# A two-layer decoder step on one core: the masked softmax copy negated and scaled, the attention blocks in another order, 32-row and 32-column tiles widened to 128, the last sums of squares collected in PSUM

## The chip, the cores and the metric

The kernel runs on one NeuronCore of a Trainium2 chip. Five engines work side by side, each on its own queue: TensorE (PE in the profile; its weight loads are PEld), VectorE (DVE), ScalarE (ACT), GpSimd (POOL) and SyncE (SP), which issues nearly all DMAs. The metric is the device time of one execution in microseconds (us), the median of repeated executions.

## The reference

One step of a small hybrid decoder, D = 1024, for 512 prompt tokens and 8 sequences of 8 sample tokens. What matters, cut:

```
x = x + g1 * (recurrent_block(modulate(rms_norm(x))))        # layer 0
x = x + g2 * swiglu(modulate(rms_norm(x)))
k, v = rope/split(modulate(rms_norm(x)) @ w_kv)               # shared keys and values
q = rope(modulate(rms_norm(x)) @ w_q)                         # layer 1, 16 heads of 64, 4 kv heads
s = where(mask, (q . k) / 8, -1e30)                           # window of 128
m = max(max(s), sink);  e = exp(s - m)
p = e / (sum(e) + exp(sink - m));  o = p @ v
x = x + g1 * (o @ w_o)
x = x + g2 * swiglu(modulate(rms_norm(x)))
y = rms_norm(x)                                               # and the state and k/v windows
```

rms_norm divides by sqrt(mean(x^2) + 1e-6) over the 1024 channels of a token and multiplies by a gain.

## The kernel before, in words

Channels lie on the 128 partitions, tokens on the columns. The tokens are cut into two halves A (h = 0) and B (h = 1) of HC = 288 columns each: 256 prompt tokens and 32 sample tokens (4 sequences of 8). x[h] holds 8 chunks of 128 channels. Every large product splits its operands into a rounded high part and a rest and does three passes of 128x128 weights against 288 columns (product, line 982; the products of the second feed-forward have an own form, lines 1293 and 1351). Those products are most of the program.

The order of all instructions is made when the kernel is built: each call on T, V, S, G or Q (TensorE, VectorE, ScalarE, GpSimd, SyncE) only records an operation with its reads and writes; schedule (line 213) then places the operations one by one, by a table of estimated costs, the place in the record (its priority, which early(n) moves forward by n), and free buffers, at most 24 candidates deep on an engine. All instructions therefore carry line 447, and the groups are told apart by the names of their tiles: mm and ada are PSUM tiles, wh weights, h the normalised input, sl, ta, tb, td working tiles, acc the running sum of squares, tst and stat small statistics.

The places that the change touches:

- stats and spread (lines 793 and 802), run for both halves ahead of the first feed-forward, of the k/v projection and of the second feed-forward; spread also runs twice at the very start. stats sums acc over the channels with three small products against a column of ones (tokens 0 to 127, 128 to 255, and the 32 sample tokens, the last as a 128x32 tile), two VectorE instructions scale them into tst. spread raises them to the power -1/2 on GpSimd and brings them from partitions to columns with three transposes; the third works on a tile of 32 rows.
- The attention stage. Its order is the string ATT (line 53): q0A is the query projection of chunk 0 (two heads) for half A, a0A the attention of that chunk (attn_chunk, line 1566), s0A a block of sample attention (attn_sample, line 1646), fA the end of half A's attention (attn_fin, line 1745, with k_out, line 1726, which writes out new keys), o0A the output projection. A chunk does its scores, the softmax, and leaves transposes and the product with V to a second part that runs one block later. Per chunk VectorE copies four score tiles out of PSUM while it adds the mask, and takes each row's maximum (tensor_tensor_reduce); for each of two column blocks two small instructions make the negated maximum and the sink's exponent (lines 1592 to 1594); then ScalarE's Exp.
- sink_setup (line 1443) prepares the sinks; evac_v (line 1488) transposes the new values, the sample part from a 128x32 tile to partitions 0 to 31.
- The end: final_chunk (line 1787) transposes each finished chunk of x (two 128x128 tiles, one 128x32) and multiplies by the final gain; final_norm (line 1801) squares the last chunk, adds its column sums to those of acc in three PSUM tiles, and then for each of three token tiles scales, raises to -1/2, multiplies the two halves of the row on VectorE and ScalarE, and issues one DMA for each half. square (line 782) adds a chunk's squares to acc on VectorE.
- residual (line 1008) adds a product to x; out (line 1351) runs the last projection of a feed-forward.

Of the kernel before, what the change touches and what calls it, by code (L numbers as in the profile page):

```python
# [52 lines left out]
ATT = ("q0A a0A q1A q2A q0B a1A q1B a0B a2A q3A q2B a1B a3A q3B q4A q4B a2B q5A a4A a3B q6A a5A q5B a4B "  # L53
       "q7A a6A q6B a5B s0A s1A a7A s2A s3A q7B s0B a6B fA a7B o0A s1B s2B o1A s3B o2A fB")
# [419 lines left out]
def trunk_kernel(ctx, tc, a):  # L474
# [17 lines left out]
    def aux():  # L492
        return ps()
# [308 lines left out]
    def spread(h, r0=0):  # L802
# [205 lines left out]
    def residual(h, o, c, g, last):  # L1008
# [6 lines left out]
        if last and (g != L1 + G2 or c < KC - 1):  # L1015
            square(h, c)
# [160 lines left out]
    def ffn(l, g, after):  # L1177
# [173 lines left out]
        def out(k, m, h):  # L1351
# [6 lines left out]
            residual(h, o, m, g, last)  # L1358
# [84 lines left out]
    def sink_setup():  # L1443
        raw, sinks, nsink, sinkS = snk[:, 0:16], snk[:, 16:32], snk[:, 32:48], snk[:, 48:51]
        A["sinks"], A["nsink"], A["sinkS"] = sinks, nsink, sinkS
# [6 lines left out]
        for g in range(2):  # L1452
            V.tensor_copy(sinks.rearrange("p (g l j) -> p g l j", g=2, l=4)[:, g], sv[:, g])
            V.tensor_scalar(nsink.rearrange("p (g l j) -> p g l j", g=2, l=4)[:, g], sv[:, g], -1.0, None, ALU.mult)
        V.tensor_scalar(sinkS[:, 1:2], sinkS[:, 0:1], 8.0, None, ALU.mult)
        V.tensor_scalar(sinkS[:, 2:3], sinkS[:, 0:1], -1.0, None, ALU.mult)
# [31 lines left out]
    def evac_v(gp):  # L1488
        def f(h, o):
# [6 lines left out]
            T.transpose(t[0:32, 2 * P : 3 * P], u.f[:, HP:HC], ident[:])  # L1496
# [7 lines left out]
            V.tensor_copy(vs[h][0:32, gs], t[0:32, 2 * P : 3 * P])  # L1504
            for b in range(4):
                Q.dma_start(
                    a["sample_v"][4 * h + b, P - NT : P].rearrange("t g d -> t (g d)")[:, gs],
                    vs[h][b * NT : (b + 1) * NT, gs],
# [57 lines left out]
    def attn_chunk(c):  # L1566
# [3 lines left out]
        def run(h):  # L1570
# [10 lines left out]
            mx, nm, den, rd = [st[:, 4 * i : 4 * i + 4] for i in range(4)]  # L1581
            e = [(ta(), tb()) for _ in range(2)]
            masks, sinks, nsink = A["masks"], A["sinks"], A["nsink"]
            for b, W in enumerate(wide):
                i = slice(2 * b, 2 * b + 2)
# [416 lines left out]
```

## Time and profile before

| what | value |
|---|---|
| median of 3 runs | 1262.38 us (1261.91 to 1264.16) |
| the profiled execution's own time | 1263.01 us |
| its span, first to last instruction | 1261.2 us |
| TensorE busy | 1237.8 us, 98% of the span |
| VectorE, ScalarE, GpSimd busy | 920.3, 663.1, 252.7 us |
| mean granted TensorE clock | 0.995 |
| chain that ended last | TensorE 86%, VectorE 6%, ScalarE 4%, DMA 2% |

A matmul's end is modelled, and a matmul is in flight while its successors run, so the busy time of TensorE hides small losses; the distance from one start to the next tells what a matmul really holds. The idle time of an engine off the chain costs nothing.

### The profile page before, as it was taken

To read this page: it belongs to the slowest core of one execution; us is meant where nothing else is said; L and a number is where in the kernel's file an instruction comes from. 1 tells how busy PE (TensorE), PEld (TensorE's weight loads), DVE (VectorE), ACT (ScalarE), POOL (GpSimd) and SP (SyncE) were. 2 spreads that over 40 slices of the span, in tenths; PEclk is the share of its full clock that TensorE was granted. 3 is DMA by queue.
4 is the path that set the end of the run, shared out by engine and by line. 5 is a ranking of instruction groups with operands and counts; after the bars stand their busy time and mean duration, and the time that the engine had idled before them with its cause. 6 is when DMAs were issued, how large, how long until landed. Compare 5 with 4: busy or idle time off the path is not lost.

```text
span 1261.2 us, 25276 instructions
## 1 busy us (share of the span) xinstructions
PE 1237.8 (98%) x9532; PEld 1166.9 (93%) x9532; DVE 920.3 (73%) x2283; ACT 663.1 (53%) x1498; POOL 252.7 (20%) x542
## 2 busy tenths in 40 slices
PE   7999999999999999999999999999999999999997
PEld 5798999899899899989998997999999999999997
DVE  6998784795577468656778887558957865875776
ACT  4788973764255335514567678538523542552442
POOL 3456351101100010011024335100011011001011
PEclk8999999999999999999999999999999999999999
DMA  9955554535456655464513220332342232332322
GB/s 306 318 179 188 188 177 151 170 86 171 140 152 191 185 167 184 156 194 137 167 33 75 68 60 27 111 97 97 85 133 68 84 110 76 90 100 80 100 69 76
DMA packets 219755, 165.38 MB, mean 131 GB/s; under 512 B 23629, under 2 KB 204841, under 8 KB 219602
## 3 DMA queue, kind: packets, MB, share of 16 engines
q1 hardware_dynamic: 219186, 163.45, 43.0%
q8 instruction: 75, 1.23, 0.4%
q0 software_dynamic: 448, 0.32, 0.1%
q14 instruction: 46, 0.38, 0.1%
HBM read 160.85 MB, written 4.87 MB: 131 GB/s over the span
## 4 chain that ended last, share of the span: by engine, by line
PE 86%; DVE 6%; ACT 4%; DMA 2%; POOL 1%; issue 1%; SPq 0%; ACTq 0%; DVEq 0%
PE mm L447 82%; PE ada L447 4%; DVE wh L447 1%; DVE ta L447 1%; ACT tb L447 1%; DVE sl L447 1%; ACT ta L447 1%; DVE tb L447 1%; ACT h L447 1%; DMA raw<-in_rnn_w_in_dram 1%; ACT wh L447 1%; POOL h L447 1%; DMA reg<-in_ada_w_dram 1%; ACT sl L447 1%; DMA reg<-in_x_prompt_dram 1%
## 5 line engine op out<-in xcount | busy, mean ns | idle before, releaser
L447 PE MATMUL mm<-h,wh 128*128 128x288 f32 x4128 | 596.2, 298 | 3.8 <-ACT h L447 1.8
L447 PEld LDWEIGHTS mm<-h,wh 128*128 128x128 f32 x4128 | 560.5, 188 | 23.2 <-issue 11.3
L447 PE MATMUL mm<-sl,wh 128*128 128x288 f32 x3218 | 460.6, 296 | 0.4 <-ACT sl L447 0.3
L447 ACT CAST wh<-raw 128x512 fp32r<-128x512 f32 (+2 forms) x380 | 269.1, 721 | 345.7 <-PE mm L447 208.9
L447 PEld LDWEIGHTS mm<-sl,wh 128*128 128x128 f32 x3218 | 436.6, 188 | 9.0 <-issue 5.9
L447 DVE TENSOR_TENSOR wh<-raw,wh 128x512 fp32r<-128x512 f32 (+2 forms) x380 | 310.2, 828 | 59.3 <-ACT wh L447 57.0
L447 DVE SCALAR_TENSOR_TENSOR x<-mm,mods,x 128x256 f32<-128x256 f32 x160 | 77.0, 482 | 136.1 <-PE mm L447 136.0
L447 POOL TENSOR_TENSOR td<-td,td 128x288 f32<-128x288 f32 x38 | 35.5, 934 | 475.8 <-ACT td L447 467.7
L447 POOL TENSOR_TENSOR x<-x,ta 128x32 f32<-128x32 f32 x152 | 55.3, 364 | 331.1 <-DVE ta L447 325.9
L447 PE MATMUL mm<-tb,wh 128*128 128x288 f32 (+1 forms) x488 | 88.5, 296 | 0.4 <-ACT td L447 0.4
L447 PEld LDWEIGHTS mm<-tb,wh 128*128 128x128 f32 x488 | 72.4, 188 | 1.9 <-DVE sl L447 0.8
L447 ACT COPY td<-mm 128x288 f32<-128x288 f32 (+2 forms) x140 | 49.0, 364 | 37.7 <-DVE mm L447 18.0
L447 DVE TENSOR_TENSOR raw<-raw,raw 128x512 f32<-128x512 f32 x76 | 61.4, 808 | 0.9
L447 PE MATMUL mm<-ta,wh 128*128 128x288 f32 (+1 forms) x254 | 56.1, 298 | 0.0
L447 ACT ACTIVATE ta<-x 128x288 f32<-128x288 f32 x56 | 24.8, 444 | 55.6 <-POOL x L447 52.4
L447 DVE TENSOR_TENSOR raw<-raw 128x512 f32<-128x512 f32 x76 | 52.2, 688 | 1.1
L447 DVE TENSOR_TENSOR td<-mm,td 128x288 f32<-128x288 f32 x76 | 34.5, 454 | 23.4 <-PE mm L447 23.3
L447 PE MATMUL ada<-reg,cz 128*32 128x512 f32 (+1 forms) x448 | 49.5, 553 | 0.0
L447 PEld LDWEIGHTS mm<-ta,wh 128*128 128x128 f32 x254 | 41.7, 188 | 1.8 <-ACT wh L447 0.8
L447 ACT ACTIVATE ta<-ta,stat 128x128 f32<-128x128 f32 (+2 forms) x72 | 32.3, 471 | 18.5 <-DVE stat L447 17.7
L447 DVE TENSOR_TENSOR acc<-acc,ta 128x288 f32<-128x288 f32 x54 | 25.1, 464 | 12.4 <-ACT ta L447 12.4
L447 ACT CAST sl<-ta 128x288 fp32r<-128x288 f32 x54 | 23.0, 431 | 18.5 <-DVE ta L447 18.5
(202 smaller groups left out, 1197.9 us busy)
## 6 DMA issues: line engine op xcount, KB each, us to landing
raw<-in_ffn_w_in_dram SPq DMA_DIRECT2D x88, 512.0 KB
reg<-in_ada_w_dram SPq DMA_DIRECT2D x80, 512.0 KB
raw<-in_ffn_w_out_dram SPq DMA_DIRECT2D x48, 384.0 KB
raw<-in_rnn_w_in_dram SPq DMA_DIRECT2D x16, 512.0 KB
reg<-in_kv_ada_w_dram SPq DMA_DIRECT2D x16, 512.0 KB
wh<-in_ada_w_dram SPq DMA_DIRECT2D x24, 256.0 KB
raw<-in_rnn_w_out_dram SPq DMA_DIRECT2D x8, 512.0 KB
raw<-in_ffn_w_out_dram SPq DMA_DIRECT2D x8, 512.0 KB
```

The costliest lines, as they stand in the source:

```text
L447: self.rec.add(eng, lambda: getattr(obj, name)(*map(real, args), **{k: real(v) for k, v in kw.items()}), cost, outs, ins, func, lat, port, ...
```

## The change

Five things, in one diff:

1. In the softmax the masked copy multiplies by -1/8 and takes the minimum, starting from the negated sink (a value per partition, read through a pointer). It so leaves -m itself; the two small VectorE instructions of each column block go, one subtraction for the whole chunk comes, and Exp gets scale -1. In the sample blocks one small instruction goes.
2. The string ATT has another order.
3. Tiles of 32 rows or 32 columns become 128 wide: the third sum in stats, the third transpose in spread, the sample part of the transposes in evac_v, attn_sample and final_chunk. The sample tokens then come out on partitions 96 to 127 (TAIL) instead of 0 to 31, and what reads them follows. stats has one VectorE instruction instead of two.
4. k_out transposes the new keys of both halves and all heads at once (one transpose and one copy instead of four of each).
5. At the end the squares of chunk 6 are no longer added to acc; acc, they and the squares of chunk 7 are summed by nine small products into one PSUM tile. One VectorE instruction scales it, two GpSimd instructions raise it, and each token tile leaves by one DMA instead of two. The last residual and this block move forward by 60 places in the record.

The core of the diff:

```diff
-ATT = ("q0A a0A q1A q2A q0B a1A q1B a0B a2A q3A q2B a1B a3A q3B q4A q4B a2B q5A a4A a3B q6A a5A q5B a4B "
-       "q7A a6A q6B a5B s0A s1A a7A s2A s3A q7B s0B a6B fA a7B o0A s1B s2B o1A s3B o2A fB")
+ATT = ("q0A q1A a0A a1A q2A q0B q1B q2B a0B q3A a2A q4A a3A a1B q3B a2B q5A a4A q4B a3B q6A a5A q5B a4B "
+       "q7A a6A s0A q6B a7A s1A s2A s3A a5B q7B s0B a6B fA o0A s1B a7B s2B s3B o1A o2A fB")
...
-    TOK = [slice(0, P), slice(P, 2 * P), slice(2 * P, HC)]
+    late_square = [None, None]
+
+    TOK, TAIL = [slice(0, P), slice(P, 2 * P), slice(HC - P, HC)], slice(P - 32, P)
...
-            T.matmul(pt[0 : ts.stop - ts.start, t : t + 1], acc[h][:, ts], ones, start=True, stop=True)
-        V.tensor_scalar(st[:, 0:2], pt[:, 0:2], 1.0 / D, EPS, ALU.mult, ALU.add)
-        V.tensor_scalar(st[0:32, 2:3], pt[0:32, 2:3], 1.0 / D, EPS, ALU.mult, ALU.add)
+            T.matmul(pt[:, t : t + 1], acc[h][:, ts], ones, start=True, stop=True)
+        V.tensor_scalar(st, pt[:, 0:3], 1.0 / D, EPS, ALU.mult, ALU.add)
         spread(h)
...
-        for t, ts in enumerate(TOK):
-            r = slice(r0, r0 + 32) if t == 2 else ALL
-            T.transpose(o[:, ts], rs[r, t : t + 1].to_broadcast([r.stop - r.start, P]), ident[r, r])
+        for t, n0 in ((2, HP - r0), (0, 0), (1, P)):
+            T.transpose(o[:, n0 : n0 + P], rs[:, t : t + 1].to_broadcast([P, P]), ident[:])
...
-        if last and (g != L1 + G2 or c < KC - 1):
+        if last and g == L1 + G2 and c == KC - 2:
+            late_square[h] = s = ta()
+            S.activation(s.f[:, 0:HC], x[h][:, c, :], AF.Square)
+        elif last and (g != L1 + G2 or c < KC - 1):
             square(h, c)
...
-            residual(h, o, m, g, last)
+            with early(60 if last and l == 1 and m == KC - 1 else 0):
+                residual(h, o, m, g, last)
...
             for b, W in enumerate(wide):
-                i = slice(2 * b, 2 * b + 2)
                 for j in range(2):
-                    y = e[b][j].f
-                    V.tensor_tensor_reduce(out=y[:, 0:W], in0=sc[j][:, 256 * b : 256 * b + W], in1=masks[:, 256 - W : 256], op0=ALU.add, op1=ALU.max,
-                                           scale=1.0, scalar=-1e30, accum_out=mx[:, 2 * b + j : 2 * b + j + 1])
-                V.scalar_tensor_tensor(nm[:, i], mx[:, i], -0.125, nsink[:, 2 * c : 2 * c + 2], ALU.mult, ALU.min)
-                V.tensor_tensor(mx[:, i], nm[:, i], sinks[:, 2 * c : 2 * c + 2], ALU.add)
+                    k, y = 2 * b + j, e[b][j].f
+                    V.tensor_tensor_reduce(out=y[:, 0:W], in0=sc[j][:, 256 * b : 256 * b + W], in1=masks[:, 256 - W : 256], op0=ALU.add, op1=ALU.min,
+                                           scale=-0.125, scalar=nsink[:, 2 * c + j : 2 * c + j + 1], accum_out=nm[:, k : k + 1])
                 for j in range(2):
-                    y = e[b][j].f[:, 0:W]
-                    S.activation(y, y, AF.Exp, bias=nm[:, 2 * b + j : 2 * b + j + 1], scale=0.125, accum_out=den[:, 2 * b + j : 2 * b + j + 1])
-
-            S.activation(mx, mx, AF.Exp)
-            V.tensor_tensor(den, den, mx, ALU.add)
+                    k, y = 2 * b + j, e[b][j].f[:, 0:W]
+                    S.activation(y, y, AF.Exp, bias=nm[:, k : k + 1], scale=-1.0, accum_out=den[:, k : k + 1])
+            nk2 = nsink[:, 2 * c : 2 * c + 2].unsqueeze(1).to_broadcast([P, 2, 2])
+            V.tensor_tensor(sk.rearrange("p (b j) -> p b j", b=2), nm.rearrange("p (b j) -> p b j", b=2), nk2, ALU.subtract)
+            S.activation(sk, sk, AF.Exp)
+            V.tensor_tensor(den, den, sk, ALU.add)
...
-                T.transpose(t[0:32, P : 2 * P], e.f[:, P:W], ident[:])
+                T.transpose(t[:, P : 2 * P], e.f[:, W - P : W], ident[:])
...
-                V.tensor_copy(pn[:, :, bl, :], t[0:32, P : 2 * P].rearrange("p (g n) -> p g n", g=2))
+                V.tensor_copy(pn[:, :, bl, :], t[TAIL, P : 2 * P].rearrange("p (g n) -> p g n", g=2))
...
     def k_out(h):
+        if h == 0:
+            t = aux()
+            T.transpose(t[:, 0:P], A["nk"].rearrange("p g h n -> p (g h n)"), ident[:])
+            nkT.append(sl())
+            S.copy(nkT[0].f[:, 0:P], t[:, 0:P])
         for gp in range(2):
-            t = aux()
-            T.transpose(t[0:32, 0:P], A["nk"][:, gp, h, :], ident[:])
-            ko_ = sl()
-            ko = ko_.f[0:32, 0:128]
-            S.copy(ko, t[0:32, 0:P])
...
-        T.transpose(t[0:32, 2 * P : 3 * P], x[h][:, c, HP:HC], ident[:])
+        T.transpose(t[:, 2 * P : 3 * P], x[h][:, c, TOK[2]], ident[:])
...
+        for i, r in enumerate((ALL, ALL, TAIL)):
+            V.tensor_tensor(yt[h][i][r, cs], t[r, i * P : (i + 1) * P], gfin[r, cs], ALU.mult)
...
+        with early(60):
+            w = ta()
+            S.activation(w.f[:, 0:HC], x[h][:, KC - 1, :], AF.Square)
+            pt = aux()
+            st, rs = tst[h][:, 0:3], tst[h][:, 3:6]
+            sums = (acc[h], late_square[h].f, w.f)
+            for i, y in enumerate(sums):
+                for t, ts in enumerate(TOK):
+                    T.matmul(pt[:, t : t + 1], y[:, ts], ones, start=i + t == 0, stop=i == 2, skip_group_check=True)
+            late_square[h].done()
+            w.done()
+            V.tensor_scalar(st, pt[:, 0:3], 1.0 / D, EPS, ALU.mult, ALU.add)
+            G.tensor_tensor(rs[:, 0:1], st[:, 0:1], mhalf[:, 0:1], ALU.pow)
+            G.tensor_tensor(rs[:, 1:3], st[:, 1:3], mhalf[:, 1:3], ALU.pow)
         for t in range(3):
...
+            y = yt[h][t][r, :]
+            if t < 2:
+                Q.dma_start(a["y_prompt"][0, h * HP + t * P : h * HP + (t + 1) * P, :], y)
+            else:
+                Q.dma_start(a["y_sample"][4 * h : 4 * h + 4].rearrange("b t d -> (b t) d"), y)
```

## Rows read from the trace of the kernel before

**Rows 1.** Stretches: length, busy us (count) of PE, PEld, DVE, ACT, POOL; clock, DMA, GB/s.

```profile
692.00:770.00 78.00, 76.13 (x666) 68.41 (x666) 65.67 (x279) 57.39 (x190) 32.86 (x73) 1.00 0.22 55
770.00:812.00 42.00, 40.76 (x339) 34.37 (x340) 28.95 (x129) 28.63 (x107) 14.77 (x40) 1.00 0.30 85
812.00:1250.00 438.00, 437.58 (x3298) 435.76 (x3297) 315.06 (x674) 197.56 (x412) 46.70 (x92) 1.00 0.30 90
1250.00:1261.20 11.20, 3.72 (x27) 2.85 (x26) 4.89 (x21) 2.83 (x5) 1.91 (x4) 0.78 0.30 105
```

**Rows 2.** TensorE in order of time (start, length, idle), around one stats and spread.

```profile
843.57 0.69 PE L447 MATMUL mm<-small,acc 128*128 128x1 f32 x6
844.19 1.60 PE L447 MATMUL mm<-h,wh 128*128 128x288 f32 x10
845.63 0.55 PE L447 MATMUL mm<-ident,tst 128*128 128x128 f32 x3
846.11 2.12 PE L447 MATMUL mm<-h,wh 128*128 128x288 f32 x14
```

**Rows 3.** TensorE in order of time, last projection with final_chunk's transposes.

```profile
1246.12 0.38 PE L447 MATMUL mm<-ident,x 128*128 128x128 f32 x2
1246.26 0.77 PE L447 MATMUL mm<-sl,wh 128*128 128x288 f32 x4
1246.87 0.27 PE L447 MATMUL mm<-ident,x 128*32 128x128 f32 x1
1246.90 1.96 PE L447 MATMUL mm<-sl,wh 128*128 128x288 f32 x13
```

**Rows 4.** VectorE in order of time, inside one chunk's softmax.

```profile
723.21 0.16 DVE L447 SCALAR_TENSOR_TENSOR stat<-stat,snk 128x2 f32<-128x2 f32 x1
723.28 0.42 DVE L447 CUSTOM_DVE_ANT_0 tb<-mm,reg 128x256 f32<-128x256 f32 x1
```

**Rows 5.** VectorE groups by shape, 690 to 830: busy us, mean ns, idle before, releasers.

```profile
L447 DVE SCALAR_TENSOR_TENSOR x<-mm,mods,x 128x256 f32<-128x256 f32 x9 | 4.3, 483 | 7.9 <-PE mm L447 7.9
L447 DVE TENSOR_TENSOR h<-ada,h 128x256 fp32r<-128x256 f32 x4 | 1.7, 420 | 0.7 <-ACT h L447 0.6
```

**Rows 6.** Waits of TensorE, 640 to 812: total us, times, longest.

```profile
PE mm L447 <- DVE td L447: 0.5, 2, 0.3
PE mm L447 <- ACT td L447: 0.4, 2, 0.2
```

**Rows 7.** All engines in order of time, the last ten microseconds.

```profile
1251.60 0.18 DVE L447 TENSOR_TENSOR ta<-mm,mods 128x32 f32<-128x32 f32 x1
1251.70 0.28 DVE L447 TENSOR_TENSOR h<-mm,h 128x128 f32<-128x128 f32 x1
...
1252.66 0.17 DVE L447 TENSOR_TENSOR x<-x,ta 128x32 f32<-128x32 f32 x1
1252.92 0.44 ACT L447 ACTIVATE ta<-x 128x288 f32<-128x288 f32 x1 [1.19 <-DVE x L447]
...
1253.42 0.76 PE L447 MATMUL mm<-small,ta 128*128 128x1 f32 x6
1253.48 0.67 DVE L447 TENSOR_TENSOR h<-mm,h 128x128 f32<-128x128 f32 x3 [0.65 <-PE mm L447]
1254.08 0.28 DVE L447 TENSOR_SCALAR tst<-mm 128x1 f32<-128x1 f32 x3
1254.29 1.66 POOL L447 TENSOR_TENSOR tst<-tst,small 128x1 f32<-128x1 f32 x3 [3.03 <-DVE tst L447]
...
1254.88 1.95 ACT L447 ACTIVATE h<-h,tst 128x512 f32<-128x512 f32 x3 [1.51 <-POOL tst L447]
1255.39 1.82 SPq L447 DMA_DIRECT2D out_y_prompt_dram<-h  x4
1257.30 1.16 SPq L447 DMA_DIRECT2D out_y_sample_dram<-h  x2
```

**Rows 8.** GB/s that all DMAs moved, 1255.0 to 1261.2, 40 equal slices of 0.155 us.

```profile
GB/s 0 0 0 0 0 0 0 13 330 383 383 410 331 357 423 396 383 357 383 383 410 384 383 344 396 304 278 251 251 80 0 0 0 0 0 0 0 0 0 0
```

More of the change, by code (lines that the diff above doesn't have):

```diff
@@ L1495, in f @@
                 T.transpose(t[:, b * P : (b + 1) * P], u.f[:, b * P : (b + 1) * P], ident[:])
-            T.transpose(t[0:32, 2 * P : 3 * P], u.f[:, HP:HC], ident[:])
+            T.transpose(t[:, 2 * P : 3 * P], u.f[:, TOK[2]], ident[:])
             u.done()
@@ L1670, in run @@
             st = new_stat()
-            mx, nm, den, rd = st[:, 0:1], st[:, 1:2], st[:, 2:3], st[:, 3:4]
+            nm, den, rd = st[:, 0:1], st[:, 1:2], st[:, 2:3]
             e = ta()
-            V.tensor_tensor_reduce(out=e.f[:, 0:W], in0=o[:, 0:W], in1=masks[:, 256 + W * bl : 256 + W * (bl + 1)], op0=ALU.add, op1=ALU.max,
-                                   scale=1.0, scalar=-1e30, accum_out=mx)
             G.tensor_copy(e.f[:, W : W + 1], sinkS[:, 1:2])
-            V.scalar_tensor_tensor(nm, mx, -0.125, sinkS[:, 2:3], ALU.mult, ALU.min)
-            S.activation(e.f[:, 0 : W + 1], e.f[:, 0 : W + 1], AF.Exp, bias=nm, scale=0.125, accum_out=den)
+            V.tensor_tensor_reduce(out=e.f[:, 0:W], in0=o[:, 0:W], in1=masks[:, 256 + W * bl : 256 + W * (bl + 1)], op0=ALU.add, op1=ALU.min,
+                                   scale=-0.125, scalar=sinkS[:, 1:2], accum_out=nm)
+            S.activation(e.f[:, 0 : W + 1], e.f[:, 0 : W + 1], AF.Exp, bias=nm, scale=-1.0, accum_out=den)
             V.reciprocal(rd, den)
@@ L1697, in second @@
                 for gp in range(2):
-                    T.matmul(av[:, 256 * gp : 256 * gp + 256], vs[h][0:32, gp * P : (gp + 1) * P], pn[:, gp].rearrange("p b n -> p (b n)"), start=False, stop=True, skip_group_check=True)
+                    T.matmul(av[:, 256 * gp : 256 * gp + 256], vs[h][TAIL, gp * P : (gp + 1) * P], pn[:, gp].rearrange("p b n -> p (b n)"), start=False, stop=True, skip_group_check=True)
                 for j, r in enumerate(HALF):
@@ L1801, in final_norm @@
     def final_norm(h):
-        w = ta()
-        S.activation(w.f[:, 0:HC], x[h][:, KC - 1, :], AF.Square)
-        pt = [aux()[0 : ts.stop - ts.start, 0:1] for ts in TOK]
-        st, rs = tst[h][:, 0:3], tst[h][:, 3:6]
-        for i in range(2):
-            for o, ts in zip(pt, TOK):
-                T.matmul(o, (acc[h], w.f)[i][:, ts], ones, start=i == 0, stop=i == 1)
-        w.done()
+        with early(60):
[12 more added lines that the diff above has]
+            G.tensor_tensor(rs[:, 1:3], st[:, 1:3], mhalf[:, 1:3], ALU.pow)
@@ L1843, in x_half @@
                 V.tensor_scalar(tst[0][0:32, 2:3], y[0:32], 1.0 / D, EPS, ALU.mult, ALU.add)
-                V.tensor_scalar(tst[1][32:64, 2:3], y[32:64], 1.0 / D, EPS, ALU.mult, ALU.add)
+                V.tensor_scalar(y, y, 1.0 / D, EPS, ALU.mult, ALU.add)
         V.tensor_scalar(st[:, 0:2], st[:, 0:2], 1.0 / D, EPS, ALU.mult, ALU.add)
```

45 lines of the change are left out of this document (19 added, 26 removed).

## The prediction

> **What bounds the kernel now.** I read the profile in this order. First the page: TensorE is busy 98% of the span and carries 86% of the chain that ended last, so time can be won in two ways only, by taking TensorE's own time away or by closing its idle time. Second the stretches [rows 1], to see where that idle time is. From 812 to 1250 it is 0.4 us in 438, with one matmul started every 0.133 us (438 / 3298); the attention, 692 to 812, has 1.87 + 1.24 = 3.1 us; from 1250 on TensorE is busy 3.7 of 11.2 us, a tail in which one step waits for the other. VectorE is at 84% from 692 to 770 and has 25 us free over the attention's 120 (120 - 65.67 - 28.95). Third TensorE in order of time around the sums of squares, where starts show what a tile really holds [rows 2, 3]. Fourth the softmax [rows 4 to 6] and fifth the tail [rows 7, 8].
>
> **The change part by part.**
>
> *Sums and transposes of 128 rows (stats, spread).* The three transposes of spread hold 0.48 us (845.63 to 846.11), and the products behind them start late: fourteen take 2.12 us, where thirteen behind a lone transpose take 1.96, so 0.16 for one product of 0.133, 0.03 more than that transpose's own after-cost [rows 2, 3]. That after-cost is 0.08: four products behind a pair take 0.61 us instead of 0.53. So spread costs 0.48 + 0.11 = 0.59. A pair of 128x128 transposes among products costs 0.14 + 0.08 = 0.22, 0.11 each, and three 0.33. What goes is the change to a 32-row tile, 0.26 us, at six places (both halves, three norms): 1.6 us. The two at the very start stand before the bulk of the products; I take nothing for them. The six sums of stats hold 0.62, and the ten products behind them 1.44 instead of 1.33: 0.73 [rows 2]. At 0.11 each six full ones are 0.66; the trace has no set of six full ones, so 0 to 0.13 per place, and I take 0.07, by the transposes: 0.4 us. One VectorE instruction fewer there shortens a chain that runs behind products: nothing, and where the k/v stage does wait for the norm it only helps that the saved time is not lost again.
>
> *32-column tiles widened (final_chunk, evac_v, attn_sample).* A 128x32 transpose between products costs 0.03 (1246.87 to 1246.90) and then the same 0.08: 0.11, as a full one [rows 3]. Sixteen, four and eight of them are worth nothing. The Trainium skill, "TensorEngine Tiling (Array Packing)", section Key Properties, says that a change of tiling mode drains TensorE; the 32-row tile shows it, the 128x32 transposes do not. If each of these 28 paid like a 32-row tile (0.26), 7.3 us more would go; that is a rival below. The sample tokens now lie on partitions 96 to 127, and the last product of a half's sample attention reads its 32 rows there; no row shows that place, two sets of four matmuls, between -0.2 and +0.2 us, taken at 0. On VectorE the evacuations from there follow ones from partition 0. Today three run in 0.67 us though one takes 0.28, so they overlap by 0.08 [rows 7]. The Trainium skill, "VectorE: DVE Perf Modes", section Two Vector instructions with no wait between them, has an instruction that starts in another quadrant of partitions held until all earlier ones are through. By it each of these loses its overlap twice, 0.16 us; sixteen in the last stage are 2.6 us of VectorE's time, hidden where VectorE has 123 us free in 438 [rows 1], but the last one stands in the tail: the sum would be 0.2 us worse.
>
> *k_out.* Three of four transposes go, 3 x 0.11 = 0.3 us of TensorE in the attention. The sixteen small DMAs stay.
>
> *Softmax.* Per chunk three small VectorE instructions go; one holds 0.07 us (723.21 to 723.28) [rows 4], so 16 x 3 x 0.07 and 8 x 0.07 for the sample blocks: 3.9 us less. Each of 72 masked copies now reads a pointer; the trace has none of that form, so the nearest rows bound it: a two-input instruction of 256 columns with a pointer takes 483 ns, one without 420 [rows 5], 0 to 0.06 each, 0 to 4.5 us. I take the upper end: VectorE's time stays as it was (+0.6), and its free 25 us cover it. The latency shrinks: Exp of a first copy waits today for the second copy (0.42) and the small instruction (0.16) [rows 4]; now for its own copy, about half a microsecond sooner in sixteen chunks. Worth what TensorE waits for its results, the transposed probabilities in td: 0.5 + 0.4 us [rows 6]. I take 0.8.
>
> *Order of the blocks.* The order is worked out from costs and priorities, so every block's neighbours change and the trace cannot price it. Bounds: all of the 3.1 us of idle closed, or as much again and more opened (below). I take 0 beyond the 0.8, since the query products that fill are the same number and only move earlier for B.
>
> *The end.* The last sample add starts at 1252.66 though its input is ready at 1251.78 [rows 7]; ahead of it VectorE does an evacuation, the sum into acc and two more evacuations. With the sum gone and the block moved forward it starts at about 1251.85, 0.8 us sooner, and with it Square (1252.92) and the last sums (1253.42 to 1254.18). Today the scaling waits besides for evacuations until 1254.08; then only for the sums, some 1253.45. Raising to -1/2 for the first token tile (0.55, a third of 1.66) ends at 1254.1 instead of 1254.85. From there the first DMA goes at 1255.39 today, 0.54 later, when VectorE's half is through; with one DMA for a whole row it waits for ScalarE's half too, 0.65 to 0.72 (a third of 1.95 or more), so 0.85 later, 1254.95. That is 0.45 sooner. SP issues three DMAs instead of six: its last starts at 1256.3 and ends near 1256.8, where today it ends at 1258.46. But the 1.18 MB flow at about 380 GB/s from 1256.2 on almost without a break [rows 8], so the bytes decide and not the issues: 0.45, and some 0.15 from the last five slices, which run at 250 to 300 GB/s behind the two small DMAs. Taken 0.6; bounds 0 (the larger pieces start later) and 1.4 (three issues of 0.46, 1.82 / 4).
>
> *Sum.* 1.6 + 0.4 + 0.3 + 0.8 + 0.6 = 3.7 us. Against the profiled execution's 1263.01 that is 1259.3. The median of the runs shown is 0.63 below that execution, so 1258.7.
>
> **Rivals.** *Only part arrives.* At the k/v boundary TensorE waits for ScalarE and VectorE soon after, and time saved before a wait is waited out; if half of 2.0 us goes so and the 0.8 of the softmax do not show, the gain is 1.0 + 0.3 + 0.6 = 1.9 us, 1260.5, no change that can be told. For it: TensorE idles in the attention. Against it: four of the six places stand in stretches like 812 to 1250 with hardly any idle time [rows 1].
>
> *The order closes the attention's waits*: 2.3 us more than counted, 1256.4. For it: a0A's first softmax now has three query products of A and three of B around it. Against: a third of that idle time lies in the sample blocks, which still stand together.
>
> *Every narrow tile cost a drain*: 7.3 us more, 1251.4, by the page on tiling named above; the rows on the 128x32 transposes speak plainly against it [rows 3].
>
> *Slower: the sample blocks lie open.* At the end of the attention a7B no longer stands between fA and o0A, and s1A to s3A and s2B, s3B follow each other; each is a chain over TensorE, ScalarE, VectorE and GpSimd, and o0A needs all of A's. Today eight sample blocks and the two ends idle 1.24 us in 770 to 812 [rows 1], 0.12 each. Without softmax gain the rest of the change saves 2.9. If each of the ten waits 0.41 us or more, that is gone; from 0.66 on the kernel is slower by 0.2%. At 0.75 it is 6.3 - 2.9 = 3.4 us slower, 1265.8. Against it: all o-products of A wait for the same end, but B's query products and a6B are still there to fill.
>
> **How the numbers follow.** 0.2%, 2.5 us, is about what a measurement of this kernel can tell from no change. Forecast (gain of 2.2 to 5 us) 0.46, of which 0.07 lie under 2.5; part only 0.24, of which 0.04 reach 2.5; order closes the waits 0.13; drains 0.03; slower 0.14. Faster: 0.39 + 0.04 + 0.13 + 0.03 = 0.59; same: 0.07 + 0.20 = 0.27; slower 0.14. The range: below, the 1256.4 with the tail at its upper bound (0.8 more) and some of the sums' bound, 1255.2; above, no gain at all and a good part of the slower case, 1264.0.
>
> **What would show it.** Right: three transposes of spread in about 0.25 us with the products 0.08 late behind them, at six places; the same 0.11 for final_chunk's third transpose; idle time of TensorE in the attention at 2 to 2.5 us; masked copies of about 0.48 us; the last sample add straight behind its input, a first output DMA some 0.45 us sooner after the last product, and three of them. Wrong: masked copies so slow that VectorE runs full in the attention; waits of TensorE around fA and o0A; idle time at the k/v boundary grown by what the sums saved; an output flow that starts later because one large DMA waits for both halves.

## The result and the profile after

The changed kernel takes 1267.05 us (median; 1265.72 to 1267.99), the kernel before beside it on the same chip 1263.1 us. The ratio is 1.0031, interval 1.0021 to 1.0040: slower by 0.31%, where 1258.7 was forecast and 1264.0 was the upper end of the range. The profiled spans are 1264.7 and 1261.2 us.

Where it went is read from the same work in both traces. Every kernel here has 8472 wide products (matmuls that move 288 columns or more). The table gives the time between the starts of numbered ones, worked out from the trace's start times: in us, the profiled execution of each kernel. The six runs beside before and after are explained below.

| from, to product | stage | before | after | e8 | e13 | e10 | e11 | e12 | e17 |
|---|---|---|---|---|---|---|---|---|---|
| start, 50 | loads | 43.64 | 42.61 | 43.45 | 45.27 | 42.19 | 42.32 | 42.89 | 43.26 |
| 50, 4500 | up to the k/v projection | 600.63 | 601.01 | 600.75 | 600.80 | 601.26 | 600.54 | 601.14 | 600.65 |
| 4500, 5350 | attention | 182.37 | 182.68 | 183.23 | 182.39 | 184.82 | 195.66 | 180.22 | 180.12 |
| 5350, 8300 | second feed-forward | 395.39 | 394.76 | 395.08 | 395.09 | 395.37 | 395.39 | 394.77 | 394.78 |
| 8300, 8460 | last stage | 27.39 | 29.88 | 29.37 | 27.42 | 27.39 | 27.42 | 27.42 | 27.66 |
| 8460, 8471 | last products | 1.45 | 3.45 | 2.00 | 1.54 | 1.45 | 1.46 | 1.45 | 1.54 |
| 8471, end | tail | 10.37 | 10.33 | 11.10 | 9.76 | 10.38 | 10.15 | 10.16 | 10.27 |

The first two lines differ from run to run by more than any edit does (e10 and before are the same code there, 42.19 and 43.64); nothing is read from them. The lines below them scatter less, but they do: e8 and e13 are the kernel before up to 1223 us, and e8 reads 183.23 in the attention for 182.37, and both read 0.3 less than before behind it. In e8 most of the difference is the granted clock (the last column but two), before and then e8:

```profile
786.00:790.00 4.00, 3.77 (x26) 2.60 (x25) 2.82 (x15) 3.59 (x14) 1.15 (x2) 1.00 0.52 150
```

```profile
786.00:790.00 4.00, 4.00 (x19) 2.38 (x18) 2.70 (x13) 3.60 (x14) 1.15 (x2) 0.58 0.48 138
```

0.58 on average is mostly 1.2 GHz instead of 2.4, and the products there fall back by 0.7 us. So a difference under 0.9 us in the attention, or 0.3 behind it, tells nothing between two single executions.

After against before: +0.3 in the attention, which holds the softmax, k_out and two of the six places of the sums, and where 1.8 less was forecast (0.8 + 0.3 + 2 x 0.33); -0.6 behind it, with two more places, where 0.7 less was; +2.5 and +2.0 in the last 30 us of products, where nothing was forecast; 0 in the tail, where 0.6 less was.

The stretches of after, answering [rows 1] (length, busy us and count of PE, PEld, DVE, ACT, POOL; granted clock, DMA, GB/s):

```profile
692.00:770.00 78.00, 75.98 (x667) 67.77 (x669) 62.39 (x235) 56.94 (x194) 37.53 (x77) 1.00 0.21 55
770.00:812.00 42.00, 40.81 (x341) 35.17 (x339) 29.82 (x118) 27.91 (x99) 14.74 (x37) 1.00 0.30 84
812.00:1250.00 438.00, 436.87 (x3289) 434.45 (x3288) 315.51 (x662) 197.62 (x411) 45.69 (x90) 1.00 0.30 90
1250.00:1264.70 14.70, 6.18 (x46) 5.32 (x44) 6.75 (x24) 3.44 (x6) 1.73 (x4) 0.78 0.22 80
```

The attention's idle time is what it was (2.0 + 1.2 us). VectorE has 3.3 us less to do in 692 to 770 (0.9 more in 770 to 812), and TensorE gained nothing by it. In 812 to 1250 TensorE's idle time rose from 0.4 to 1.1 us.

The last stage, 1222 to 1256. First what the weight loads of TensorE wait for in the kernel before (total us, times, longest):

```profile
PEld mm L447 <- DVE x L447: 0.5, 2, 0.3
```

and VectorE's evacuations of the final chunks there (groups by shape: busy us, mean ns, idle before):

```profile
L447 DVE TENSOR_TENSOR h<-mm,h 128x128 f32<-128x128 f32 x32 | 7.9, 284 | 1.8 <-PE mm L447 1.7
...
L447 DVE TENSOR_TENSOR h<-mm,h 32x128 f32<-32x128 f32 x16 | 4.3, 269 | 0.0
```

The same two views of the changed kernel:

```profile
PEld mm L447 <- DVE x L447: 2.9, 6, 1.1
```

```profile
L447 DVE TENSOR_TENSOR h<-mm,h 128x128 f32<-128x128 f32 x30 | 7.3, 284 | 2.8 <-PE mm L447 2.8
...
L447 DVE TENSOR_TENSOR h<-mm,h 32x128 f32<-32x128 f32 x15 | 4.5, 297 | 0.2
```

The sample evacuation from partitions 96 to 127 is 28 ns longer, and TensorE waits 2.4 us more for x, the residual's result, which it is to transpose (the longest of the six waits, 1.1, lies behind the last product, as 0.3 does in the kernel before; ahead of it they are 1.8 us against 0.2). The end of after in order of time, answering [rows 7]:

```profile
1252.30 0.79 DVE L447 TENSOR_TENSOR h<-mm,h 128x128 f32<-128x128 f32 x3
...
1252.52 0.80 PE L447 MATMUL mm<-small,acc 128*128 128x1 f32 x6
...
1253.18 0.81 PE L447 MATMUL mm<-small,ta 128*128 128x1 f32 x6
...
1253.92 0.78 PE L447 MATMUL mm<-sl,wh 128*128 128x288 f32 x4
1254.20 0.80 DVE L447 TENSOR_TENSOR h<-mm,h 128x128 f32<-128x128 f32 x3 [1.11 <-PE mm L447]
1255.03 0.48 DVE L447 SCALAR_TENSOR_TENSOR x<-mm,mods,x 128x256 f32<-128x256 f32 x1
...
1255.65 0.19 DVE L447 TENSOR_TENSOR x<-x,ta 128x32 f32<-128x32 f32 x1
1255.88 0.44 ACT L447 ACTIVATE ta<-x 128x288 f32<-128x288 f32 x1 [3.33 <-DVE x L447]
1256.37 0.83 PE L447 MATMUL mm<-small,ta 128*128 128x1 f32 x6
...
1258.82 1.00 SPq L447 DMA_DIRECT2D out_y_prompt_dram<-h  x2
```

Three evacuations take 0.79 to 0.80 us, where they took 0.67 [rows 7]. Twelve sums now stand on TensorE ahead of the last four products. The last residual (1255.03) waits for three evacuations, so the sample add stands 1.25 us behind the last product (1255.65 against 1254.40), where it stood 1.79 behind (1252.66 against 1250.87) [rows 7]; the first output DMA is issued 4.42 behind it instead of 4.52, since from the add to this DMA 3.17 us pass instead of 2.73.

### The profile page after: what moved, and what is told of

It reads as the page before. It is cut to its first block, busy times and chain, and to the rows that moved or that the text cites. A ratio compares the mean times of both kernels' runs of the same rounds, so it can differ in the third digit from the quotient of the medians.

```text
span 1264.7 us, 25237 instructions
## 1 busy us (share of the span) xinstructions
PE 1240.1 (98%) x9541; PEld 1168.8 (92%) x9541; DVE 921.2 (73%) x2213; ACT 663.3 (52%) x1494; POOL 256.4 (20%) x539
## 4 chain that ended last, share of the span: by engine, by line
PE 83%; DVE 10%; ACT 3%; issue 2%; POOL 1%; DMA 0%; ACTq 0%; POOLq 0%; DVEq 0%; SPq 0%
PE mm L447 79%; PE ada L447 4%; DVE sl L447 2%; DVE ta L447 2%; DVE wh L447 2%; DVE h L447 1%; DVE tb L447 1%; ACT ta L447 1%; ACT sl L447 1%; ACT h L447 0%; ACT tb L447 0%; DVE x L447 0%; DVE acc L447 0%; DVE td L447 0%; ACT L447 0%
## 5 line engine op out<-in xcount | busy, mean ns | idle before, releaser
L447 ACT ACTIVATE ta<-ta,stat 128x256 f32<-128x256 f32 (+2 forms) x72 | 32.2, 470 | 16.8 <-DVE stat L447 15.4
```

Source lines behind the costliest of these rows:

```text
L447: self.rec.add(eng, lambda: getattr(obj, name)(*map(real, args), **{k: real(v) for k, v in kw.items()}), cost, outs, ins, func, lat, port, ...
```

## The experiments

Each was timed beside the kernel before on one chip. The first four split the last stage.

**e1_no_early**: the changed kernel, with the sums at their own place.

```diff
-            with early(60 if last and l == 1 and m == KC - 1 else 0):
+            with early(0):
...
-        with early(60):
+        with early(0):
```

> The changed kernel with nothing moved forward at its end (both shifts of 60 places in the record set to 0). Theory one, order: in the changed kernel twelve small sums (six of acc, six of chunk 6's squares, 1.34 us from 1252.52 to 1253.86) and a transpose stand ahead of the last four products on TensorE, and the output can't begin before these; putting them back behind the products should end the last product 1.4 to 2.0 us sooner (at 1252.4 to 1253.0 us instead of 1254.4) and the kernel at a ratio to the one before of 1.0015 to 1.0020. Theory two, held VectorE instructions: the triples of evacuations stay at 0.80 us instead of 0.67 and the transposes go on waiting for them, so the ratio stays within 0.0005 of 1.0031.

1265.98 us, ratio 1.0029 (1.0020 to 1.0039). The last eleven products take 1.79 us instead of 3.45, so it is the sums that hold them up; but the tail grows to 10.89, and 8300 to 8460 stays at 29.81. The order of the sums is not the main loss.

**e2_one_quadrant**: the changed kernel in the same order, sample evacuations of all 128 rows, so that each of the three starts at partition 0.

```diff
-        for i, r in enumerate((ALL, ALL, TAIL)):
+        for i, r in enumerate((ALL, ALL, ALL)):
```

> The changed kernel, but the evacuation of the sample part in the last stage takes all 128 partitions, from partition 0 on, instead of partitions 96 to 127 alone. The order of the instructions on every engine is the same. Theory two, held VectorE instructions: three evacuations go from 0.80 us back to 0.67, TensorE's waits for the new x in 1222 to 1250 (0.15 + 0.25 + 0.2 + 0.39 + 0.56 = 1.5 us beyond the normal distance) close, the ratio falls by 0.0012 to 0.0025. Theory one, order: the waits come from where the transposes stand and not from the evacuations' length, no change, ratio 1.0028 to 1.0034.

1264.61 us, ratio 1.0013 (1.0004 to 1.0022). Four times the rows, and faster: triples take 0.68 us, 8300 to 8460 takes 27.80. The last eleven products still take 3.18.

**e3_no_early_one_quadrant**: both edits.

> Both edits together, on the changed kernel. If the two causes add up, they take 3 to 4 us and the ratio is 1.0000 to 1.0008; the last product then starts at about 1250.5 to 1251.5 us. If only one of them is at work, the ratio is that of the run with this one alone.

1262.88 us, ratio 1.0003 (0.9994 to 1.0011). Both together take back most of what the last stage had lost: from product 8300 to the end it takes 40.07 us, where after takes 43.66 and before 39.21.

**e4_last_stage_of_before**: the changed kernel with residual, final_chunk and final_norm as before.

```diff
-        T.transpose(t[:, 2 * P : 3 * P], x[h][:, c, TOK[2]], ident[:])
+        T.transpose(t[0:32, 2 * P : 3 * P], x[h][:, c, HP:HC], ident[:])
...
-        for i, r in enumerate((ALL, ALL, TAIL)):
+        for i, n in enumerate((P, P, 32)):
...
-            sums = (acc[h], late_square[h].f, w.f)
...
```

> The changed kernel with the whole last stage of the kernel before (narrow third tiles, squares of chunk 6 added to acc, three PSUM tiles, six DMAs, nothing moved forward); softmax, order of blocks, stats, spread, values and keys as changed. The milestones of the two traces agree that the changed kernel is 0.97 us ahead at the 8300th product, before the last stage. So the ratio should be 0.9990 to 0.9996 (1.0 us less than before). If it is 1.002 or more, the loss was not in the last stage.

1262.37 us, ratio 0.9994 (0.9985 to 1.0003). So all of the change ahead of the last stage is worth about 0.06%, and no gain at all lies within the interval, where I had 3.1 us, 0.25%. The next four ask why.

**e5_sums_alone**: the kernel before with the new stats and spread only.

```diff
-        V.tensor_scalar(st[:, 0:2], pt[:, 0:2], 1.0 / D, EPS, ALU.mult, ALU.add)
-        V.tensor_scalar(st[0:32, 2:3], pt[0:32, 2:3], 1.0 / D, EPS, ALU.mult, ALU.add)
+        V.tensor_scalar(st, pt[:, 0:3], 1.0 / D, EPS, ALU.mult, ALU.add)
...
+            T.transpose(o[:, n0 : n0 + P], rs[:, t : t + 1].to_broadcast([P, P]), ident[:])
...
```

> The kernel before with only the sums of squares and spread on full tiles (six places; the last stage, the softmax and the order of blocks as before). By the prediction's terms 1.6 + 0.4 = 2.0 us less, a ratio of 0.9984. By the rival read from the trace of after (the saving per place is 0.15 to 0.25 on the transposes, nothing on the sums, and some of it is waited out soon after): 0.4 to 1.0 us less, a ratio of 0.9992 to 0.9997. The three transposes of spread hold 0.25 to 0.33 us in both; what tells them apart is how far the products 300 us later have moved: 2.0 us by the first, at most 1.0 by the second.

1262.39 us, ratio 0.9997 (0.9988 to 1.0006), the rival's; the 0.9984 of the prediction lies outside the interval. At the place of [rows 2], TensorE of the changed kernel in order of time (e5 has the same lines some 0.04 us sooner):

```profile
843.24 0.77 PE L447 MATMUL mm<-small,acc 128*128 128x1 f32 x6
843.87 1.44 PE L447 MATMUL mm<-h,wh 128*128 128x288 f32 x9
845.20 0.54 PE L447 MATMUL mm<-ident,tst 128*128 128x128 f32 x3
845.50 2.78 PE L447 MATMUL mm<-h,wh 128*128 128x288 f32 x19
```

The sums hold 0.63 us as before. The transposes hold 0.30 (845.20 to 845.50) and not 0.25. And nine products stand in front of them where ten did, so that TensorE reaches them just as GpSimd's power ends (845.14) and loses about 0.1. By the products behind them the six places of e5 save 0.16, 0.12, 0.26, 0.20, 0.17 and 0.12 us, 1.03 in all, and within the next 12 us products fall back by 0.10, 0.18, 0.29, 0.07 and 0.18, 0.82 in all.

**e7_softmax_alone**: the kernel before with the new softmax only (the old order of blocks).

```diff
-                                           scale=1.0, scalar=-1e30, accum_out=mx[:, 2 * b + j : 2 * b + j + 1])
+                                           scale=-0.125, scalar=nsink[:, 2 * c + j : 2 * c + j + 1], accum_out=nm[:, k : k + 1])
...
```

> The kernel before with only the new softmax (masked copy scaled and lowered from the negated sink on, in prompt chunks and sample blocks; order of blocks, tiles and last stage as before). By the prediction 0.8 us less in the attention (Exp starts half a microsecond sooner): a ratio of 0.9994. By the rival read from the trace of after (each masked copy is 0.06 us longer and the chain Exp, reciprocal, probabilities is no shorter where the next copies queue on VectorE): 0 to 0.4 us more, a ratio of 1.0000 to 1.0003. The wait of TensorE on results of the softmax between 640 and 812 us tells them apart: under 2.5 us in all by the first, 3.5 or more by the second; masked copies of 256 columns at 0.48 us in both.

1277.02 us, ratio 1.0111 (1.0097 to 1.0125). Neither expectation came near: 14 us lost, 13.4 of them in the attention (195.78 us for products 4500 to 5350). The edit changes the planner's order too: from 717.7 us on TensorE's instructions stand in another order than in the kernel before.

**e8_sample_at_96_alone**: the kernel before, its last stage in its own order, with the sample evacuation on the last quadrant.

```diff
-        T.transpose(t[0:32, 2 * P : 3 * P], x[h][:, c, HP:HC], ident[:])
+        T.transpose(t[:, 2 * P : 3 * P], x[h][:, c, HC - P : HC], ident[:])
...
-        for i, n in enumerate((P, P, 32)):
-            V.tensor_tensor(yt[h][i][0:n, cs], t[0:n, i * P : (i + 1) * P], gfin[0:n, cs], ALU.mult)
+        for i, r in enumerate((ALL, ALL, TAIL)):
+            V.tensor_tensor(yt[h][i][r, cs], t[r, i * P : (i + 1) * P], gfin[r, cs], ALU.mult)
...
```

> The kernel before with one thing changed in its last stage: the sample tokens' evacuation of each final chunk reads and writes partitions 96 to 127 instead of 0 to 31 (with it the transpose of 128 columns and the sums of the sample tokens); sums after the last product, six output DMAs, as before. If the held evacuation costs what one quadrant gave back, 1.3 to 2.1 us more before the last product and up to 0.2 behind it: a ratio of 1.0011 to 1.0018, triples of evacuations of 0.79 us instead of 0.67 and more than 1 us of TensorE waiting for transposes' input x. If the held evacuation is hidden as the prediction had it, since VectorE has time to spare there and the sums don't stand ahead of the last products: within 0.2 us of before, triples of 0.79 us all the same, and TensorE waits for x under 0.6 us.

1266.39 us, ratio 1.0029 (1.0020 to 1.0038): this one edit costs about as much as the whole change, and more than the 1.0018 that I expected at most. In its trace 3.3 us of that lie behind product 8300 (1.98 + 0.55 + 0.73). First VectorE in the kernel before, then in e8, where TensorE's weight load stands last:

```profile
1243.79 0.67 DVE L447 TENSOR_TENSOR h<-mm,h 128x128 f32<-128x128 f32 x3
1244.38 0.46 DVE L447 SCALAR_TENSOR_TENSOR x<-mm,mods,x 128x256 f32<-128x256 f32 x1
```

```profile
1246.76 0.79 DVE L447 TENSOR_TENSOR h<-mm,h 128x128 f32<-128x128 f32 x3
1247.56 0.46 DVE L447 TENSOR_TENSOR acc<-acc,ta 128x288 f32<-128x288 f32 x1
1248.04 0.80 DVE L447 TENSOR_TENSOR h<-mm,h 128x128 f32<-128x128 f32 x3
1248.87 0.48 DVE L447 SCALAR_TENSOR_TENSOR x<-mm,mods,x 128x256 f32<-128x256 f32 x1
1249.27 0.18 DVE L447 TENSOR_TENSOR ta<-mm,mods 128x32 f32<-128x32 f32 x1
1249.41 0.20 PEld L447 LDWEIGHTS mm<-ident,x 128*128 128x128 f32 x2 [0.61 <-DVE x L447]
```

VectorE works without a gap for 2.6 us here: two triples, each 0.12 us longer than before. From the start of a triple to that of the next instruction it is even 0.21 more (1246.76 to 1247.56 against 1243.79 to 1244.38), since the next one no longer overlaps with it. Then comes the residual, for which the next transposes on TensorE wait, and behind these, in order, all products.

**e9_old_order_and_last_stage**: e4 with the string ATT of before.

```diff
-ATT = ("q0A q1A a0A a1A q2A q0B q1B q2B a0B q3A a2A q4A a3A a1B q3B a2B q5A a4A q4B a3B q6A a5A q5B a4B "
+ATT = ("q0A a0A q1A q2A q0B a1A q1B a0B a2A q3A q2B a1B a3A q3B q4A q4B a2B q5A a4A a3B q6A a5A q5B a4B "
...
```

> The changed kernel with the last stage of before and the old order of attention blocks: only full tiles, k_out and softmax are new. The same with the new order gave 0.9994. If the new order opens waits in the attention (products 4500 to 5350 came 0.3 to 0.4 us later in every run that has it), this is 0.3 to 0.8 us faster than that, a ratio of 0.9988 to 0.9992. If the order is worth nothing, as the prediction has it, 0.9994 again, and the 0.3 to 0.4 us stay. If the new order is what saved the rest, 1.0000 or more.

1269.81 us, ratio 1.0055 (1.0041 to 1.0069), against 0.9994 with the new string and nothing else different: the new order of blocks is worth 0.6%, 6.8 us of the attention (189.57 against 182.78). I had put it at 0. The new string alone on the kernel before was not tried.

The next four keep an order and change what stands in it.

**e10_pointer_alone**: the kernel before, every instruction in its place, with a pointer in the masked copies.

```diff
-                                           scale=1.0, scalar=-1e30, accum_out=mx[:, 2 * b + j : 2 * b + j + 1])
+                                           scale=1.0, scalar=nsink[:, 2 * c + j : 2 * c + j + 1], accum_out=mx[:, 2 * b + j : 2 * b + j + 1])
...
```

> The kernel before with one operand changed: the 72 masked copies start their maximum from a value in SBUF (the negated sink) instead of from the constant -1e30; every instruction and its order on every engine stay. The shift that the softmax takes out is then at least the negated sink, which changes nothing in its result. By the prediction's upper end, 72 x 0.06 = 4.3 us of VectorE hidden under its free 25 us: a ratio of 1.0000, products behind the attention within 0.3 us of before. If the longer copies lie in the chain that TensorE waits for, 1 to 4 us more in the attention: 1.001 to 1.003.

1265.11 us, ratio 1.0019 (1.0010 to 1.0028). The copies on VectorE between 640 and 830 us, before and then e10:

```profile
L447 DVE CUSTOM_DVE_ANT_0 ta<-mm,reg 128x256 f32<-128x256 f32 x24 | 10.0, 418 | 3.3 <-PE mm L447 3.2
```

```profile
L447 DVE CUSTOM_DVE_ANT_0 ta<-mm,reg,snk 128x256 f32<-128x256 f32 x24 | 11.4, 476 | 2.8 <-PE mm L447 2.8
```

0.06 us each, as the upper end had it; 72 of them make 4.3 us of VectorE, and 2.45 of these arrive at TensorE, in some ten steps of 0.1 to 0.4 us between 714 and 791 us. TensorE's waits, 640 to 850, name who is late, before and then e10:

```profile
PE mm L447 <- ACT ta L447: 0.8, 1, 0.8
...
PE mm L447 <- DVE stat L447: 0.2, 1, 0.2
```

```profile
PE mm L447 <- ACT ta L447: 1.3, 2, 0.8
...
PE mm L447 <- DVE stat L447: 0.8, 2, 0.4
```

**e11_softmax_no_pointer**: e7 in the same order, minimum started from a constant. The softmax then takes out a shift that leaves the sink aside; the sink's own term uses the same shift, so the result stays that of a softmax.

```diff
-                                           scale=-0.125, scalar=nsink[:, 2 * c + j : 2 * c + j + 1], accum_out=nm[:, k : k + 1])
+                                           scale=-0.125, scalar=1e30, accum_out=nm[:, k : k + 1])
...
```

> The new softmax alone, as in the run that gave 1.0111, with the minimum started from a constant instead of the negated sink: no pointer, every instruction and its order on every engine as in that run. If the 0.06 us longer copies are what the attention cannot bear in that order (the order was worked out with copies of the old length), most of the 14 us goes: 1.000 to 1.003. If it is the order itself, which comes out another way once the small instructions are gone, it stays at 1.008 to 1.011.

1274.99 us, ratio 1.0090 (1.0076 to 1.0103): the order, not the pointer. The attention takes 195.66 us, where e7 took 195.78; the 2 us by which the two medians differ lie in the loads of their profiled executions (42.32 and 44.39), so this pair says nothing of the pointer. Stretches of TensorE (length, busy us and count, granted clock, DMA, GB/s):

```profile
790.00:812.00 22.00, 20.51 (x164) 0.92 0.49 137
812.00:835.00 23.00, 19.64 (x112) 0.78 0.16 46
```

and TensorE in order of time there, with the idle time before each:

```profile
816.69 0.44 PE L447 MATMUL mm<-ident,ta 128*128 128x128 f32 x2 [1.39 <-POOL ta L447]
817.51 1.12 PE L447 MATMUL mm<-td,reg 128*128 128x64 f32 x4 [0.38 <-DVE td L447]
822.21 13.00 PE L447 MATMUL mm<-h,wh 128*128 128x288 f32 x78 [1.59 <-ACT h L447]
```

At the end of the attention TensorE stands idle, and the granted clock falls: 0.78 on average in 812 to 835, so a part of it at 1.2 GHz instead of 2.4. Before, the same stretch has 174 matmuls at full clock, here 112. From 640 to 835 TensorE is idle for 10.4 us, before for 4.3; the clock takes at most 1.8 + 5.1 us (0.08 x 22 and 0.22 x 23, an estimate from the rows above). The 13.3 us that the attention lost are thus about half waiting and half clock. e9, with the old string too but at 1.00 throughout the attention, loses 6.8. Why the planner's order comes out so without the small instructions was not settled.

**e12_new_order_no_pointer**: e4 with the edit of e11.

> The changed kernel with the last stage of before (0.9994 in its run) and the minimum of the masked copies started from a constant: no pointer, the order on every engine as in that run. If the pointer costs the attention there too, 1 us or more less: 0.9984 or below, and the wait of TensorE for the softmax's results (ACT ta, 2.3 us in that run) falls below 1.5. If the longer copies are hidden, 0.9994 again and the wait stays.

1259.83 us, ratio 0.9967 (0.9955 to 0.9980), faster than both kernels. The wait for ACT ta falls from 2.3 to 1.6 us, not below the 1.5 that I expected; the attention takes 180.22 us, 2.6 less than e4.

**e13_sample_at_96_later**: e8 with each chunk's transposes one group of products later.

```diff
             if last and l == 1:
-                final_chunk(h, m)
+                for q in ([m - 1] if m else []) + ([m] if m == KC - 1 else []):
+                    final_chunk(h, q)
```

> The kernel before with the sample evacuations at partitions 96 to 127, as in the run that gave 1.0029, but each chunk's transposes of x come one group of products later (the last chunk's as before). The evacuations are held as before, triples of 0.79 us. If the loss comes from TensorE's queue, in which transposes stand that wait for a late residual, the weight loads' waits for x fall from 2.0 us to under 0.5 and the ratio to 1.0000 to 1.0010 (the tail may be up to 0.7 us longer, since two chunks' evacuations then come at the end). If VectorE as a whole is too slow there, 1.002 to 1.003 again.

1262.55 us, ratio 0.9995 (0.9986 to 1.0004). Weight loads' waits and evacuations, the two views of above:

```profile
PEld mm L447 <- DVE x L447: 0.2, 1, 0.2
```

```profile
L447 DVE TENSOR_TENSOR h<-mm,h 32x128 f32<-32x128 f32 x16 | 4.8, 298 | 0.2
```

The evacuations are as slow as in e8, and the loss is gone. (The kernel before with the later transposes alone was not run, so what these would gain by themselves stays open.) It was not VectorE's throughput but the place of the transposes in TensorE's queue.

The last four take the three causes from the changed kernel itself. **e14_after_no_pointer**, the pointer:

```diff
...
-                                   scale=-0.125, scalar=sinkS[:, 1:2], accum_out=nm)
+                                   scale=-0.125, scalar=1e30, accum_out=nm)
```

> The changed kernel with one operand of the 72 masked copies changed (minimum started from a constant), the order on every engine as in the changed kernel. If the pointer costs there what it cost in the two pairs of runs so far (2.4 and 3.4 us), the 1.0031 falls to 1.0004 to 1.0012, and products behind the attention come 2.5 us sooner than in the changed kernel, with the last stage as slow as before (3.5 to 4.5 us lost from product 8300 to the last). If its cost was one of those orders, 1.003 again.

1264.88 us, ratio 1.0014 (1.0006 to 1.0023); the attention takes 180.15 us, 2.5 less than in after, as expected; the ratio lies a little above the expected 1.0004 to 1.0012.

**e15_after_later**, the transposes' place, the pointer left in:

```diff
-                final_chunk(h, m)
+                for q in ([m - 1] if m else []) + ([m] if m == KC - 1 else []):
+                    final_chunk(h, q)
```

> The changed kernel with the last stage's transposes one group of products later, and nothing else: sample evacuations held, pointer and early sums as in the changed kernel. If TensorE's queue behind late residuals is what the held evacuations cost (about 2 us), the weight loads' waits for x fall from 1.8 us to under 0.5 and the ratio from 1.0031 to 1.0010 to 1.0018; what the early sums cost stays. If the early sums alone make the last stage slow here, 1.0025 or more.

1264.44 us, ratio 1.0013 (1.0004 to 1.0022); 8300 to 8460 takes 27.96 instead of 29.88, the last eleven products still 3.48.

**e16_after_both**: the edits of e14 and e15.

> The changed kernel with both: no pointer, and the last stage's transposes one group of products later. If the two causes are apart from each other and are all but the early sums, the gains add: 1.0031 - 0.0024 - 0.0016 = 0.9991, between 0.9980 and 1.0000. If a further cause is left in the change, it stays at 1.0005 or more.

1262.24 us, ratio 0.9994 (0.9985 to 1.0003). 1.0031 - 0.0017 - 0.0018 is 0.9996: the two gains add.

**e17_after_both_no_early**: e16 and, as in e1, the sums at their own place.

```diff
...
-        with early(60):
+        with early(0):
```

> As the last, and with the early sums taken back too (both blocks at their own place in the order). What is left of the change is then the full tiles, k_out, the new softmax without a pointer, the new order and one DMA for each row. If nothing but the pointer, the held evacuations' place and the early sums was against the change, 0.9970 to 0.9985, near the 0.9967 of the run with the last stage of before; if one DMA for each row costs something in the tail, 0.9985 to 1.0000.

1260.33 us, ratio 0.9979 (0.9971 to 0.9988). Without the three causes the change is a gain of 0.2%, and its interval overlaps that of e12, which has the old end: nothing more of it is against it that these runs can tell.

## Why the prediction was wrong

*The step that failed most: "hidden where VectorE has 123 us free in 438".* The evacuations' price was near: 2.6 us were named, and 16 triples at 0.21 more, by the start of what follows, are 3.4. "VectorE: DVE Perf Modes", section "Two Vector instructions with no wait between them", of the Trainium skill holds an instruction whose start quadrant differs from the last one's; the traces agree (0.67 us a triple at partitions 0, 0, 0, 0.80 at 0, 0, 96, and 0.68 with 128 rows all from 0; the evacuation at 96 starts 0.01 us behind the end of the one ahead of it, where the one at 0 starts 0.08 ahead of that end). Whether the change of quadrant or the place at 96 itself slows them, no run separates. What failed is the cover. Free time was there: from 1222 to 1250 VectorE of the kernel before is busy for 21.6 of 28 us. But a sum says nothing of where the free time lies, and in this stage transposes of x stand on TensorE right behind each residual and VectorE works 2.6 us without a gap (e8). e8 and e13 show it both ways: the same slow evacuations, 1.0029 with the transposes close behind the residual, 0.9995 a group later. From the changed kernel this is 0.18% (e2 and e15 alike), 2.3 us.

*The second: "I take the upper end ... and its free 25 us cover it".* The pointer's size was right (60 ns in after, 418 to 478, where [rows 5] had 63), the cover again not: 57% of it reaches TensorE (2.45 of 4.3 us). The copies stand in the chain from scores to Exp to probabilities; with the pointer TensorE's waits for its results grow (ACT ta 0.8 to 1.3, DVE stat 0.2 to 0.8 us, e10). Price: 0.17 to 0.27% (after against e14, e10, e4 against e12), 2.5 us of the attention in all three traces.

*The third: the block moved forward.* I followed what early sums free behind the last product and not whom they pass: twelve sums, 1.3 us, stand ahead of the last four products on the same engine, and wait for their own inputs there. The tail is not shorter for it: the last residual then stands behind three evacuations, so that the sample add comes 0.54 us sooner behind the last product and not 0.8, and the way from there to the first DMA is 3.17 us, about the forecast 3.10. So 0.1 of the 0.45 is left at the first DMA, and the 0.6 of the tail was 0. Price: 0.02% (after against e1), 0.10% (e2 against e3), 0.15% (e16 against e17).

*Sums and spread, 2.0 us.* Mechanism right, size wrong. The 32-row tile does cost what was said (0.48 to 0.30 at 845), the sums gained nothing, 0 being the lower bound that I had named; and four fifths of the 1.03 us that the places save are lost again within 12 us, the rival *only part arrives* (I had taken stretches without idle time as proof against it). Of 2.0 us some 0.2 to 0.6 remain: the second feed-forward is 0.6 shorter, but e8 and e13, without the new sums, are 0.3 shorter too.

*Softmax 0.8, order 0.* Measured together with k_out and two places of the sums: +0.3 instead of -1.8. Taken apart they are far larger and of both signs: the softmax alone in the old order +13 us (e11, without pointer), the order -6.8 (e9 against e4), the pointer +2.5. These do not add up, since each was measured beside other edits and about half of the +13 is the clock. Without the pointer the attention is 1.7 to 2.3 us faster than before (e12, e14, e16, e17), about what was forecast for it. That "the trace cannot price it" was right of the order; that it was therefore taken as 0 while the softmax was priced by itself was not, since the softmax edit changes the order too.

*The rivals.* "Slower: the sample blocks lie open" did not happen: 770 to 812 idles 1.19 us, as before, and not ten times 0.41. The slower outcome came from a place that I had looked at and dismissed. Every narrow tile a drain: not so; a full third transpose holds 0.11 us in e8, as the narrow one did [rows 3]. *Output flow:* one DMA for each row changes nothing that can be told (tail 10.33 against 10.37, e17 10.27).

## What to carry to other kernels

Free time of an engine, averaged over a stage, covers nothing by itself: for each instruction that grows, look a few microseconds behind it on its own engine for the next result that an in-order TensorE waits for, and price the growth in full where the engine has no gap up to there. Where a planner makes the order, an edit that removes instructions is also an edit of the order; time it with the order held still (one operand changed, nothing moved) before believing a sum by parts. And a wait that is born of closeness can be taken away without making anything faster, by putting the reader one group of products later.

## What the runs showed of the hardware that I had not expected

- Three evacuations at partitions 0, 0 and 96 are slower (0.80 us) than three of four times the last one's rows, all from partition 0 (0.68).
- A per-partition pointer instead of a constant costs a masked copy with its minimum or maximum 57 to 60 ns at 128, 160 and 256 columns alike (284 to 344, 315 to 372 and 418 to 476 in e10).
- The granted clock fell in the attention where no instruction had changed: 0.58 on average over 786 to 790 in e8, 1.00 in the kernel before with the same order of instructions up to there; TensorE was busy for 15.4 of the 16 us ahead in both. In e11 it averages 0.92 over 790 to 812 and 0.78 over 812 to 835, where TensorE stood idle for 1.4 and 1.6 us. What makes the difference between e8 and before no run shows.
